# Attention logits from four products a head instead of six, and the bias table from split rows

## The chip, the cores and the metric

The kernel runs on one NeuronCore of a Trainium2 chip. The metric is the device time of one launch in microseconds (us). Engines named here: TensorE (matrix products; "PE" in the profile, its weight loads "PEld"), VectorE ("DVE"), ScalarE ("ACT") and SyncE ("SP", which only issues transfers). They run their own queues in order and wait for each other through semaphores.

## The reference

A small decoder: a retention layer, then an attention layer (MoBA), each with an MLP and a gated per-layer embedding, for 256 positions and a model width of 2048. The change concerns the attention logits alone. With 256 positions there is one block of keys, so each of 16 heads (width 128) attends causally over its own block:

```
l_own = einsum('hqd,hkd->hqk', qc, k_own) * scale          # scale = 128 ** -0.5
l_own = where(dist_own >= 0, l_own + bias_t[:, t5_bucket(dist_own)], NEG_INF)
probs = softmax(l_own)
```

`bias_t` is a table of 32 distance buckets by 16 heads. All arrays are float32.

## The kernel before

**Precision.** Each float32 operand x is split into a high part (a cast to float32r, which ScalarE does) and a low part (x minus the high part, VectorE); `split` (lines 217 to 219) does both. A product is then made of three: high x high, high x low, low x high.

**Units.** The whole kernel is a list of units. One unit is one 128 x 1024 piece of weights. `run` goes through the units in order: it issues the load of a later piece, splits the piece three units ahead (`conv`, tiles wh and wl, lines 218 and 219), issues the unit's products, and then the tasks that were put behind this unit with `at`. Nothing is rescheduled: the order of the Python calls is the order of every engine's queue.

**The attention layer** has four groups of four heads. With b the number of a group's first unit, units b to b+7 compute the keys (ak), b+8 to b+15 the queries (aq), b+16 to b+23 the values (av). `evac_q` adds the two halves of a query tile and splits it into qx (high part in columns 0 to 255, low part in 256 to 511); kx is the same for the keys. Behind unit b+11+2j stands `logits` for head j of the group, behind unit b+15+2j `turn`. So behind unit b+15 stand the evacuation of the last query tile, `turn` of the first head and `logits` of the third, in this order, and behind b+17 `turn` of the second head and `logits` of the fourth.

`logits` takes one PSUM bank and computes two blocks in it: queries 0 to 127 against keys 0 to 127 (t=0) and queries 128 to 255 against all keys (t=1), with three products each (lines 742 to 744). VectorE scales each block and adds the bias (line 751), takes the row maximum (752); ScalarE does the exponential and its sum (753); VectorE divides (754, 757). `turn` takes one bank, transposes the probabilities into it (line 764) and splits them from the bank into ph (ScalarE) and pl (VectorE), lines 218 and 219. The bank is free once pl is done.

**Banks.** `aux` hands out two banks in turn, to the logits, the transposes and some small products of other layers. A tile that gets a bank waits until the last reader of its former tile is done.

**The bias table.** `bias_rows` loads the table (33 x 16, tile relb) and a one-hot matrix (33 x 384, tile oh), multiplies them in float32 (line 677) and stores the rows; each group reads its part back as tile T.

Of the kernel before, what the change touches and what calls it, by code (L numbers as in the profile page):

```python
# [11 lines left out]
F32R = mybir.dt.float32r  # L12
I32 = mybir.dt.int32
AF = mybir.ActivationFunctionType
ALU = mybir.AluOpType
AX = mybir.AxisListType

P = 128
S = 256
# [5 lines left out]
AH, DH = 16, 128  # L25
# [44 lines left out]
class Core:  # L70
# [593 lines left out]
    def bias_rows(self, i):  # L664
        nc, cp, io = self.nc, self.cp, self.io
        st = {}

        def load():
            st["rb"] = cp.tile([33, AH], F32, name="relb")
            nc.vector.memset(st["rb"][32:33], NEG)  # L670
            nc.sync.dma_start(st["rb"][:32], io["rel_bias"])
            st["oh"] = self.slot("oh", (33, 384))
            nc.sync.dma_start(st["oh"], io["onehot"])

        def rows():
            ps = self.aux("bv")
            nc.tensor.matmul(ps[:AH, :384], st["rb"], st["oh"], start=True, stop=True)
            st["bv"] = self.slot("bv", (AH, 384))
            nc.vector.tensor_copy(st["bv"], ps[:AH, :384])

        def store():
            nc.scalar.dma_start(io["bvec"], st["bv"][:, None, :].to_broadcast([AH, BR, 384]))
        self.at(i, load)
        self.at(i + 6, rows)
        self.at(i + 8, store)

    def attention(self):
        nc = self.nc
        mm = nc.tensor.matmul
        first = len(self.units)  # L690
        self.at(first + 4, self.stats_a)
        self.at(first + 6, self.stats_b)
        sc = {}

        def q_scale():
            sc["s"] = self.cp.tile([P, 2], F32, name="qs")
            nc.vector.tensor_scalar_mul(sc["s"], self.rn, DH ** -0.5)
        self.at(first + 8, q_scale)
        self.ot = {}
        for g in range(AH // GH):  # L700
            b, st = len(self.units), {}

            def table(st=st, g=g):
                st["T"] = []
                bv = self.io["bvec"]
                for j in range(0, GH, 2):
                    t = self.slot("T", (P, 2, S))
                    for q in range(0, P, BR):
                        src = bass.AP(tensor=bv.tensor, offset=bv.offset + (g * GH + j) * BR * 384 + 127 - q, ap=[[383, BR], [BR * 384, 2], [1, S]])
                        nc.sync.dma_start(t[q:q + BR], src)  # L710
                    st["T"] += [t[:, 0], t[:, 1]]
            self.at(b, table)

            def evac_k(n, ps, st=st):
                t = self.small("kt")
                self.fold(t, ps)
                yield
                yield
                nc.vector.tensor_mul(t, t, self.rb)
                x = self.slot("kx", dt=F32R)  # L720
                self.split(x[:, :S], x[:, S:], t)
                st["k", n] = x

            def evac_q(n, ps, st=st):
                t = self.small("qt")
                self.fold(t, ps)
                yield
                x = self.slot("qx", dt=F32R)
                self.split(x[:, :S], x[:, S:], t)
                st["q", n] = x  # L730

            self.phase_a(f"ak{g}_", "att", g * 24, GH, 2, LEAD if g == 0 else 1, lambda k: self.xx[k], evac_k)
            self.phase_a(f"aq{g}_", "att", g * 24 + 8, GH, 2, 1, lambda k: self.x2[k], evac_q)

            def logits(j, st=st):
                ps = self.aux("lg")
                q, k = st["q", j], st["k", j]
                for t in range(2):
                    o = ps[:, :P] if t == 0 else ps[:, P:384]
                    n = P * (t + 1)  # L740
                    qh, ql = q[:, t * P:(t + 1) * P], q[:, S + t * P:S + (t + 1) * P]
                    mm(o, qh, k[:, :n], start=True, stop=False)
                    mm(o, qh, k[:, S:S + n], start=False, stop=False)
                    mm(o, ql, k[:, :n], start=False, stop=True)
                l = self.slot("lg", (P, 384))
                mx = self.cp.tile([P, 2], F32, name="mx", tag="mx", bufs=2)
                sm = self.cp.tile([P, 2], F32, name="sm", tag="sm", bufs=2)
                for t in range(2):
                    c = slice(0, P) if t == 0 else slice(P, 384)
                    bias = st["T"][j][:, P:] if t == 0 else st["T"][j]  # L750
                    nc.vector.scalar_tensor_tensor(l[:, c], ps[:, c], sc["s"][:, t:t + 1], bias, op0=ALU.mult, op1=ALU.add)
                    nc.vector.reduce_max(mx[:, t:t + 1], l[:, c], axis=AX.X, negate=True)
                    nc.scalar.activation(l[:, c], l[:, c], AF.Exp, bias=mx[:, t:t + 1], accum_out=sm[:, t:t + 1])
                nc.vector.reciprocal(sm, sm)
                for t in range(2):
                    c = slice(0, P) if t == 0 else slice(P, 384)
                    nc.vector.tensor_scalar_mul(l[:, c], l[:, c], sm[:, t:t + 1])
                st["p", j] = l

            def turn(j, st=st):  # L760
                p = st.pop(("p", j))
                ps = self.aux("pt")
                for i, (c, o) in enumerate(((0, 0), (1, 1), (2, 2))):
                    nc.tensor.transpose(ps[:, o * P:(o + 1) * P], p[:, c * P:(c + 1) * P], self.ident)
                h, l = self.slot("ph_", (P, 384), F32R), self.slot("pl_", (P, 384), F32R)
                self.split(h, l, ps[:, :384])
                st["t", j] = (h, l)

            def evac_v(banks, st=st):
                st["v"] = self.natural(banks, self.rn)  # L770

            def values(j, st=st, g=g):
                (vh, vl), (ph, pl) = st["v"], st["t", j]
                ps = self.bank("y", "y", 2)
                c = slice(j * P, (j + 1) * P)
                for t in range(2):
                    o = ps[:, :S] if t == 0 else ps[:, P:S]
                    p = slice(0, S) if t == 0 else slice(S, 384)
                    mm(o, vh[t][:, c], ph[:, p], start=t == 0, stop=False)
                    mm(o, vh[t][:, c], pl[:, p], start=False, stop=False)  # L780
                    mm(o, vl[t][:, c], ph[:, p], start=False, stop=t == 1)
                x = self.slot(f"o{g}_{j}", dt=F32R)
                self.split(x[:, :S], x[:, S:], ps[:, :S])
                self.ot[g * GH + j] = x

            self.phase_b(f"av{g}_", "att", g * 24 + 16, KD // 2, lambda k: self.xx[k], evac_v)
            for j in range(GH):
                self.at(b + 11 + 2 * j, lambda j=j, f=logits: f(j))
                self.at(b + 15 + 2 * j, lambda j=j, f=turn: f(j))
                self.at(b + 25 + j // 2, lambda j=j, f=values: f(j))  # L790

        self.project("att_o", "att_o", 0, KD // 2, lambda k: self.ot[k], self.add([G_MLP1]))
# [82 lines left out]
```

## Time and profile before

| | |
|---|---|
| median of 3 runs | 2763.4 us (2762.8 to 2763.84) |
| profiled execution | 2764.53 us, of which span 2762.7 us |
| TensorE busy | 2748.0 us (99%) |
| VectorE busy | 1682.7 us (61%) |
| ScalarE busy | 1310.3 us (47%) |
| chain that ended last | 99% TensorE |
| granted TensorE clock, mean | 0.999 |

The span runs from the first instruction to the last in one profiled execution; shares are of the span. The chain that ended last is followed back from the last instruction, each step to what it waited for. Matrix products are pipelined: the interval between two starts, not the duration of one, is what a product holds TensorE for.

### The profile page before, as it was taken

To read this page: it belongs to the slowest core of one execution; us is meant where nothing else is said; L and a number is where in the kernel's file an instruction comes from. 1 tells how busy PE (TensorE), PEld (TensorE's weight loads), DVE (VectorE), ACT (ScalarE), POOL (GpSimd) and SP (SyncE) were. 2 spreads that over 40 slices of the span, in tenths; PEclk is the share of its full clock that TensorE was granted. 3 is DMA by queue.
4 is the path that set the end of the run, shared out by engine and by line. 5 is a ranking of instruction groups with operands and counts; after the bars stand their busy time and mean duration, and the time that the engine had idled before them with its cause. 6 is when DMAs were issued, how large, how long until landed. Compare 5 with 4: busy or idle time off the path is not lost.

```text
span 2762.7 us, 34143 instructions
## 1 busy us (share of the span) xinstructions
PE 2748.0 (99%) x13802; PEld 2339.9 (85%) x13802; DVE 1682.7 (61%) x2264; ACT 1310.3 (47%) x1787; POOL 0.2 (0%) x4
## 2 busy tenths in 40 slices
PE   9999999999999999999999999999999999999998
PEld 7888888888888888888888888888888888888886
DVE  6766666655566544665556776665666445664555
ACT  5444444444445433444445655554554334544454
POOL 0000000000000000000000000000000000000000
PEclk9999999999999999999999999999999999999999
DMA  7555554555555555555565555554555555555554
GB/s 267 186 186 186 186 183 179 182 183 197 183 193 189 192 191 196 185 196 185 186 209 185 189 178 183 181 178 175 196 184 197 187 194 193 189 189 192 185 200 153
DMA packets 79307, 522.50 MB, mean 189 GB/s; under 512 B 8971, under 2 KB 12972, under 8 KB 17452
## 3 DMA queue, kind: packets, MB, share of 16 engines
q1 hardware_dynamic: 78476, 519.26, 52.9%
q10 hardware_dynamic: 672, 1.05, 0.3%
q8 instruction: 108, 1.77, 0.3%
q14 instruction: 51, 0.42, 0.0%
HBM read 517.39 MB, written 2.88 MB: 188 GB/s over the span
## 4 chain that ended last, share of the span: by engine, by line
PE 99%; DVE 0%; DMA 0%; ACT 0%; SPq 0%; issue 0%
PE up L154 17%; PE up L152 9%; PE qk L154 4%; PE ak L154 2%; PE aq L154 2%; PE qk L152 2%; PE ak L152 1%; PE aq L152 1%; PE pu L551 1%; PE xt L252 1%; PE qk L181 1%; PE y L439 1%; PE sc L417 0%; PE qk L182 0%; PE dn__11012 L192 0%; PE dn__11012 L194 0%
## 5 line engine op out<-in xcount | busy, mean ns | idle before, releaser
L219 DVE TENSOR_TENSOR wl<-raw,wh 128x1024 fp32r<-128x1024 f32 (+1 forms) x970 | 1179.9, 1222 | 659.6 <-ACT wh L218 645.3
L218 ACT CAST wh<-raw 128x1024 fp32r<-128x1024 f32 (+1 forms) x970 | 1015.1, 1051 | 718.2 <-DVE rs_y L275 29.2
L154 PE MATMUL up<-x,wh 128*128 128x512 f32 x2048 | 490.5, 391 | 0.0
L154 PEld LDWEIGHTS up<-x,wh 128*128 128x128 f32 x2048 | 376.0, 188 | 72.5
L152 PEld LDWEIGHTS up<-x,wl 128*128 128x128 f32 x2048 | 263.4, 191 | 10.4
L152 PE MATMUL up<-x,wl 128*128 128x256 f32 x2048 | 266.6, 283 | 0.0
L223 ACT COPY t<-up 128x256 f32<-128x256 f32 x128 | 47.6, 372 | 331.4 <-PE up L154 331.4
L224 DVE TENSOR_TENSOR t<-t,up 128x256 f32<-128x256 f32 x128 | 53.9, 421 | 216.6 <-ACT t L223 216.3
L154 PE MATMUL qk<-x,wh 128*128 128x512 f32 x448 | 109.9, 392 | 0.0
L154 PEld LDWEIGHTS qk<-x,wh 128*128 128x128 f32 x448 | 81.8, 188 | 15.5
L230 ACT ACTIVATE x<-xt,g 128x256 fp32r<-128x256 f32 x112 | 52.5, 478 | 53.3 <-DVE x L231 39.4
L231 DVE SCALAR_TENSOR_TENSOR x<-xt,g,x 128x256 fp32r<-128x256 f32 x112 | 52.9, 480 | 27.9 <-ACT x L230 27.6
L154 PE MATMUL aq<-x,wh 128*128 128x512 f32 x256 | 63.2, 391 | 0.0
L154 PE MATMUL ak<-x,wh 128*128 128x512 f32 x256 | 63.1, 392 | 0.0
L152 PEld LDWEIGHTS qk<-x,wl 128*128 128x128 f32 x448 | 57.4, 191 | 2.2
L152 PE MATMUL qk<-x,wl 128*128 128x256 f32 x448 | 58.1, 283 | 0.0
L511 DVE SCALAR_TENSOR_TENSOR s<-t 128x256 f32<-128x256 f32 x128 | 54.6, 426 | 4.4
L154 PEld LDWEIGHTS ak<-x,wh 128*128 128x128 f32 x256 | 46.6, 188 | 8.7
L154 PEld LDWEIGHTS aq<-x,wh 128*128 128x128 f32 x256 | 46.5, 188 | 8.6
L219 DVE TENSOR_TENSOR a<-s,a 128x256 fp32r<-128x256 f32 x128 | 53.7, 419 | 0.0
L218 ACT CAST a<-s 128x256 fp32r<-128x256 f32 x128 | 52.0, 406 | 0.0
L239 ACT ACTIVATE sq<-h 128x512 f32<-128x512 f32 x48 | 30.1, 628 | 37.4 <-DVE h L520 15.6
(1011 smaller groups left out, 4992.3 us busy)
## 6 DMA issues: line engine op xcount, KB each, us to landing
raw<-mlp_up SPq DMA_DIRECT2D x128, 1024.0 KB, 4.8
raw<-mlp_dn SPq DMA_DIRECT2D x128, 1024.0 KB, 4.8
raw<-ret_in SPq DMA_DIRECT2D x94, 1024.0 KB, 4.8
raw<-att SPq DMA_DIRECT2D x48, 1024.0 KB, 4.8
raw<-ret_out SPq DMA_DIRECT2D x32, 1024.0 KB, 4.8
raw<-ple_gate SPq DMA_DIRECT2D x32, 1024.0 KB, 4.8
raw<-att_o SPq DMA_DIRECT2D x16, 1024.0 KB, 4.8
raw<-ple_up SPq DMA_DIRECT2D x4, 1024.0 KB, 4.8
```

Of the source, the lines that this page charges most:

```text
L152: mm(ps[:, S:], wl[:, c], rhs[k][:, :S], start=False, stop=end)
L154: mm(ps, wh[:, c], rhs[k], start=first and k == 0, stop=end)
L181: m(ps, wh[:, c], x, start=u + j == 0, stop=False)
L218: self.nc.scalar.copy(dst_h, src)
L219: self.nc.vector.tensor_sub(dst_l, src, dst_h.bitcast(F32))
L223: self.nc.scalar.copy(dst, ps[:, :S])
L224: self.nc.vector.tensor_add(dst, dst, ps[:, S:])
L230: self.nc.scalar.activation(t[:, :S], src, AF.Copy, scale=gs)
L231: self.nc.vector.scalar_tensor_tensor(t[:, S:], src, gs, t[:, :S].bitcast(F32), op0=ALU.mult, op1=ALU.subtract)
L239: self.nc.scalar.activation(self.slot("sq"), self.h[c][:, t], AF.Square, accum_out=self.ssq[:, t, c:c + 1])
L252: self.nc.tensor.transpose(ps[:, o * P:(o + 1) * P], self.h[c][:, t, f * P:(f + 1) * P], self.ident)
L511: nc.vector.scalar_tensor_tensor(s, t, 0.0, t, op0=ALU.max, op1=ALU.mult)
```

## The change

The products of the high part of the queries with both parts of the keys become one: the moving operand is the whole kx tile (512 columns) for t=1, and its first 128 columns of either half (2 x 128) for t=0. Their two results stand side by side in a bank of their own, so each t takes a bank, and a head takes two. The product of the low part of the queries with the high part of the keys is added to the first half. VectorE then adds two halves: one operation with the bias as before, and a second that adds the other half to the result. For the bias table, the one-hot matrix is cast and the table is split by a new task two units before the product, which becomes two products.

```
--- before.py
+++ after.py
@@ -672,9 +672,17 @@
             st["oh"] = self.slot("oh", (33, 384))
             nc.sync.dma_start(st["oh"], io["onehot"])
 
+        def parts():
+            st["ohr"] = self.slot("ohr", (33, 384), F32R)
+            nc.scalar.copy(st["ohr"], st["oh"])
+            st["rh"], st["rl"] = (cp.tile([33, AH], F32R, name=n) for n in ("relh", "rell"))
+            self.split(st["rh"], st["rl"], st["rb"])
+        self.at(i + 4, parts)
+
         def rows():
             ps = self.aux("bv")
-            nc.tensor.matmul(ps[:AH, :384], st["rb"], st["oh"], start=True, stop=True)
+            nc.tensor.matmul(ps[:AH, :384], st["rh"], st["ohr"], start=True, stop=False)
+            nc.tensor.matmul(ps[:AH, :384], st["rl"], st["ohr"], start=False, stop=True)
             st["bv"] = self.slot("bv", (AH, 384))
             nc.vector.tensor_copy(st["bv"], ps[:AH, :384])
 
@@ -733,22 +741,24 @@
             self.phase_a(f"aq{g}_", "att", g * 24 + 8, GH, 2, 1, lambda k: self.x2[k], evac_q)
 
             def logits(j, st=st):
-                ps = self.aux("lg")
                 q, k = st["q", j], st["k", j]
-                for t in range(2):
-                    o = ps[:, :P] if t == 0 else ps[:, P:384]
-                    n = P * (t + 1)
+                pss = []
+                for t in range(2):
+                    ps, n = self.aux("lg"), P * (t + 1)
                     qh, ql = q[:, t * P:(t + 1) * P], q[:, S + t * P:S + (t + 1) * P]
-                    mm(o, qh, k[:, :n], start=True, stop=False)
-                    mm(o, qh, k[:, S:S + n], start=False, stop=False)
-                    mm(o, ql, k[:, :n], start=False, stop=True)
+                    x = k if t else k.rearrange("p (a s) -> p a s", a=2)[:, :, :P]
+                    o = ps if t else ps[:, :S].rearrange("p (a s) -> p a s", a=2)
+                    mm(o, qh, x, start=True, stop=False)
+                    mm(ps[:, :n], ql, k[:, :n], start=False, stop=True)
+                    pss.append((ps[:, :n], ps[:, n:2 * n]))
                 l = self.slot("lg", (P, 384))
                 mx = self.cp.tile([P, 2], F32, name="mx", tag="mx", bufs=2)
                 sm = self.cp.tile([P, 2], F32, name="sm", tag="sm", bufs=2)
                 for t in range(2):
                     c = slice(0, P) if t == 0 else slice(P, 384)
                     bias = st["T"][j][:, P:] if t == 0 else st["T"][j]
-                    nc.vector.scalar_tensor_tensor(l[:, c], ps[:, c], sc["s"][:, t:t + 1], bias, op0=ALU.mult, op1=ALU.add)
+                    for half, rest in zip(pss[t], (bias, l[:, c])):
+                        nc.vector.scalar_tensor_tensor(l[:, c], half, sc["s"][:, t:t + 1], rest, op0=ALU.mult, op1=ALU.add)
                     nc.vector.reduce_max(mx[:, t:t + 1], l[:, c], axis=AX.X, negate=True)
                     nc.scalar.activation(l[:, c], l[:, c], AF.Exp, bias=mx[:, t:t + 1], accum_out=sm[:, t:t + 1])
                 nc.vector.reciprocal(sm, sm)
```

TensorE's queue behind unit b+15 of the first group, before: `turn` of the first head (pt), then `logits` of the third (lg), then the first products of the values.

```order
L764 MATMUL pt<-ident,lg 128x128 x3
L742 MATMUL lg<-kx,qx 128x128 [waits DVE_49,Activation_49]
L743 MATMUL lg<-kx,qx 128x128
L744 MATMUL lg<-kx,qx 128x128 [waits DVE_49]
L742 MATMUL lg<-kx,qx 128x256
L743 MATMUL lg<-kx,qx 128x256
L744 MATMUL lg<-kx,qx 128x256
L192 MATMUL av_0__12998<-wh_12874,x_0_11957 128x512 [waits PE_49]
L193 MATMUL av_0__12998<-wl_12875,x_0_11957 128x512
```

The same place after. (Names in brackets are the engines' semaphores that an instruction waits for.)

```order
L774 MATMUL pt<-ident,lg 128x128 [waits DVE_49,PE_49]
L774 MATMUL pt<-ident,lg 128x128 x2
L751 MATMUL lg<-kx,qx 128x256 [waits DVE_49,PE_49,Activation_49]
L752 MATMUL lg<-kx,qx 128x128 [waits DVE_49]
L751 MATMUL lg<-kx,qx 128x512 [waits DVE_49]
L752 MATMUL lg<-kx,qx 128x256
L192 MATMUL av_0__13008<-wh_12882,x_0_11964 128x512
L193 MATMUL av_0__13008<-wl_12883,x_0_11964 128x512
L194 MATMUL av_0__13008<-wh_12882,x_0_11964 128x512
```

Six logits products became four, and the third of them, the first one in the head's second bank, has got a wait for VectorE.

VectorE's queue at the second head of the first group, before: from the evacuation of a query tile (qt) over the logits (lg, mx, sm) to the next weight piece and the low part of the third head's queries.

```order
L224 TENSOR_TENSOR qt<-qt,aq_2_12854 128x256 [waits Activation_49]
L751 SCALAR_TENSOR_TENSOR lg<-lg,qs,T 128x128 [waits PE_49]
L752 TENSOR_REDUCE mx<-lg 128x1 [waits DVE_49]
L751 SCALAR_TENSOR_TENSOR lg<-lg,qs,T 128x256
L752 TENSOR_REDUCE mx<-lg 128x1 [waits DVE_49]
L754 RECIPROCAL sm<-sm 128x2 [waits Activation_49]
L757 TENSOR_SCALAR lg<-lg,sm 128x128 [waits DVE_49]
L757 TENSOR_SCALAR lg<-lg,sm 128x256
L219 TENSOR_TENSOR wl_12919<-raw_12780,wh_12918 128x1024 [waits Activation_49]
L219 TENSOR_TENSOR qx<-qt,qx 128x256 [waits Activation_49]
```

The same place after.

```order
L224 TENSOR_TENSOR qt<-qt,aq_2_12862 128x256 [waits Activation_49]
L761 SCALAR_TENSOR_TENSOR lg<-lg,qs,T 128x128 [waits PE_49]
L761 SCALAR_TENSOR_TENSOR lg<-lg,qs 128x128 [waits DVE_49]
L762 TENSOR_REDUCE mx<-lg 128x1 [waits DVE_49]
L761 SCALAR_TENSOR_TENSOR lg<-lg,qs,T 128x256 [waits PE_49]
L761 SCALAR_TENSOR_TENSOR lg<-lg,qs 128x256 [waits DVE_49]
L762 TENSOR_REDUCE mx<-lg 128x1 [waits DVE_49]
L764 RECIPROCAL sm<-sm 128x2 [waits Activation_49]
L767 TENSOR_SCALAR lg<-lg,sm 128x128 [waits DVE_49]
L767 TENSOR_SCALAR lg<-lg,sm 128x256
L219 TENSOR_TENSOR wl_12928<-raw_12787,wh_12927 128x1024 [waits Activation_49]
L219 TENSOR_TENSOR qx<-qt,qx 128x256 [waits Activation_49]
```

Two operations were added, each behind the first of its block and waiting for it; the rest stands as before, behind them.

## Rows read from the trace of the kernel before

**Rows 1.** The page, part 1: busy us (share of the span), instructions.

```profile
PE 2748.0 (99%) x13802; PEld 2339.9 (85%) x13802; DVE 1682.7 (61%) x2264; ACT 1310.3 (47%) x1787; POOL 0.2 (0%) x4
```

**Rows 2.** Waits of TensorE: for whom, total us, times, longest us.

```profile
PE qk L181 <- ACT wh L218: 2.3, 1, 2.3
```

**Rows 3.** Timeline, TensorE, first group, third head: start us, us, engine, line, operation.

```profile
1608.17 0.28 PE L744 MATMUL lg<-kx,qx 128*128 128x128 f32 x1
1608.28 0.33 PE L742 MATMUL lg<-kx,qx 128*128 128x256 f32 x1
...
1608.57 0.28 PE L744 MATMUL lg<-kx,qx 128*128 128x256 f32 x1
1608.69 0.40 PE L192 MATMUL av__12998<-wh,x 128*128 128x512 f32 x1
```

**Rows 4.** Timeline around the bias table's product (line 677).

```profile
1393.75 0.39 PE L193 MATMUL dn__11013<-wl,a 128*128 128x512 f32 x1
...
1393.98 0.39 PE L194 MATMUL dn__11013<-wh,a 128*128 128x512 f32 x1
...
1395.04 0.19 PEld L192 LDWEIGHTS dn__11012<-wh,a 128*128 128x128 f32 x1 [0.64 <-issue]
1395.04 0.50 PE L192 MATMUL dn__11012<-wh,a 128*128 128x512 f32 x1
...
1395.38 0.39 PE L193 MATMUL dn__11012<-wl,a 128*128 128x512 f32 x1
```

**Rows 5.** Timeline, first group, fourth head.

```profile
1614.65 0.28 PE L744 MATMUL lg<-kx,qx 128*128 128x128 f32 x1
...
1615.18 0.56 DVE L219 TENSOR_TENSOR pl__13036<-pt,ph__13035 128x384 fp32r<-128x384 f32 x1 [0.16 <-ACT ph__13035 L218]
```

**Rows 6.** Timeline at the start of the kernel.

```profile
5.34 0.42 DVE L219 TENSOR_TENSOR wl<-raw,wh 128x256 fp32r<-128x256 f32 x1
5.82 0.29 PEld L182 LDWEIGHTS qk<-x,wl 128*128 128x128 f32 x1 [0.27 <-DVE wl L219]
```

**Rows 7.** Timeline, VectorE, first group, third head.

```profile
1608.73 0.55 DVE L219 TENSOR_TENSOR pl__12970<-pt,ph__12969 128x384 fp32r<-128x384 f32 x1
1609.20 0.34 DVE L751 SCALAR_TENSOR_TENSOR lg<-lg,qs,T 128x128 f32<-128x128 f32 x1
1609.58 0.29 DVE L752 TENSOR_REDUCE mx<-lg 128x1 f32<-128x128 f32 x1
1609.78 0.48 DVE L751 SCALAR_TENSOR_TENSOR lg<-lg,qs,T 128x256 f32<-128x256 f32 x1
1610.29 0.42 DVE L752 TENSOR_REDUCE mx<-lg 128x1 f32<-128x256 f32 x1
```

**Rows 8.** Waits of VectorE, 1596.6 to 1609.28 us: first head to third.

```profile
DVE sm L754 <- ACT lg L753: 1.3, 2, 0.7
DVE wl L219 <- ACT wh L218: 0.4, 2, 0.2
```

**Rows 9.** Timeline, VectorE, second group, second and third head.

```profile
1673.94 1.22 DVE L219 TENSOR_TENSOR wl<-raw,wh 128x1024 fp32r<-128x1024 f32 x1
1675.28 0.42 DVE L224 TENSOR_TENSOR qt<-qt,aq 128x256 f32<-128x256 f32 x1
...
1680.22 1.22 DVE L219 TENSOR_TENSOR wl<-raw,wh 128x1024 fp32r<-128x1024 f32 x1
1681.56 0.42 DVE L224 TENSOR_TENSOR qt<-qt,aq 128x256 f32<-128x256 f32 x1
1682.00 0.56 DVE L219 TENSOR_TENSOR pl__13670<-pt,ph__13669 128x384 fp32r<-128x384 f32 x1
```

**Rows 10.** Timeline, TensorE, second group, third head, second half.

```profile
1681.57 0.33 PE L742 MATMUL lg<-kx,qx 128*128 128x256 f32 x1
```

**Rows 11.** Two stretches, TensorE: us, busy us (products), clock, DMA, GB/s.

```profile
9.30:13.98 4.68, 4.68 (x15) 1.00 1.03 406
13.98:18.66 4.68, 4.68 (x27) 1.00 1.04 407
```

## The prediction

> **What bounds the kernel now.** I read the page's engine line first: TensorE is busy for 2748.0 us, 99% of the span [rows 1]. Then the list of what TensorE waited for: beyond the very first products it holds a single entry, 2.3 us at the start [rows 2], and nothing in the attention layer. So the kernel is a gapless queue of matrix products, executed in the order written. Whatever takes time out of that queue is gained in full; whatever makes a product wait is lost in full, because nothing later has slack to give it back. Third, the order in which TensorE's products wait in the changed program (shown with the change). Fourth, the timelines of TensorE and VectorE around the logits.
>
> **The products themselves.** Around the third head of the first group a logits product of 128 columns holds the queue for 0.11 us (1608.17 to 1608.28) and one of 256 columns for hardly more (1608.57 to 1608.69, 0.12); the three of the second half take 0.41 in all, with one short delay at the change of width [rows 3]. A product of 512 columns takes 0.23 (1393.75 to 1393.98) [rows 4]. The new four products (256, 128, 512, 256) then cost 0.11 + 0.11 + 0.23 + 0.11 against six times 0.11: one slot of 0.11 less per head, 16 x 0.11 = 1.8 us over the kernel. The weight loads saved (two per head) lie beside other products and are counted at nothing; were each to hold the queue for its own 0.19 us [rows 4], that is a rival below.
>
> [...]
>
> **The bias table.** The single-precision product of 384 columns stands between the last ordinary product at 1393.98 and the next at 1395.04, which itself takes 0.34 instead of 0.23 to the next [rows 4]. Its cost is 1395.04 - (1393.98 + 0.23) + 0.11 = 0.94 us. Two products of the kind used elsewhere, 384 columns at three quarters of 0.23, 0.17 each, and a restart of 0.11 make 0.45: a gain of 0.49, once (bounds: nothing, and 0.94 less 0.34). The two casts and one subtraction that make the split rows stand two units earlier on engines that are busy 47% and 61% [rows 1]; they cost nothing, and 0.7 us if they were in TensorE's way.
>
> **The new wait.** There are two banks of the kind "aux". Before, a head's logits took one; now they take both. At the third and fourth head of each group the transposes of an earlier head stand directly ahead and have just taken a bank too. So the third allocation in that unit, the 512-column product, must take the bank of those transposes and cannot start before ScalarE and VectorE have emptied it. The order shows exactly this: the 512-column product waits for VectorE there, and not at heads one and two. What must end is VectorE's subtraction pl<-pt. Behind the waiting product stands all of TensorE's work.
>
> How late is it? Before, at the fourth head, pl starts at 1615.18 and lasts 0.56, so it ends at 1615.74, while the second half, then the third product, could have started at 1614.65 [rows 5]. Waking TensorE took 0.06 us when it waited for VectorE at the start (the subtraction ends 5.34 + 0.42 = 5.76, the weight load starts at 5.82) [rows 6], and the product began 0.03 later. So the second half starts at 1615.83 instead of 1614.65 + 0.11 = 1614.76: 1.07 late. What follows is then 0.23 + 0.11 and a restart of 0.11 (the 0.34 instead of 0.23 above) against 0.41: 0.05 more. Fourth head: +1.12 us.
>
> [...]
>
> **What VectorE's extra work adds.** Each head now has four scalar-tensor-tensor operations instead of two, and each waits for the one before. In the trace the small one starts 0.38 before its successor (1609.20, 1609.58), the large one 0.51 before (1609.78, 1610.29) [rows 7]: the chain of a head grows by 0.38 + 0.51 = 0.89 us. Usually that would hide, with VectorE at 61%. It does not here. From the first head's logits to pl of the third head VectorE of the first group waits only for ScalarE's steps of the same chain: 1.3 + 0.4 us, none for TensorE [rows 8]. So two heads' growth, 1.78 us, arrives in full at pl: it ends at 1608.73 + 0.55 + 1.78 = 1611.06 instead of 1609.28 [rows 7]. With 0.09 to wake, the second half of the third head starts at 1611.15 instead of 1608.28: 2.87 late, and 0.05 for restart and the shorter remainder: +2.92. This includes shorter waits on the way (at head two the low part of its queries, itself a VectorE result, comes some 0.6 us late); they add nothing, since the end is set by VectorE's chain. At the fourth head VectorE is later by 1.78 + 0.89 less 0.16 of idle time [rows 5] = 2.51, less than TensorE's 2.92: TensorE leads again, and the +1.12 stands. First group: 4.04 us.
>
> In the second group (the third's and fourth's lists of VectorE's waits read the same) VectorE has a little slack: each row may start 0.09 before the previous one ends (1608.73 + 0.55 and 1609.20 in [rows 7]), so 1673.94 + 1.22 - 0.09 = 1675.07 against 1675.28 is 0.21 idle; 1680.22 to 1681.56 another 0.21; 1681.56 to 1682.00 another 0.11 [rows 9]. The growth reaching pl is 1.78 - 0.53 = 1.25; it ends at 1682.00 + 0.56 + 1.25 = 1683.81, the second half starts at 1683.90 instead of 1681.57 [rows 10]: 2.33, with 0.05 and 1.12 it is 3.50 a group. Three such groups: 10.50.
>
> **Sum.** 4.04 + 10.50 - 0.49 = +14.05 us; the 0.11 saved per head is inside (heads one and two gain nothing, as VectorE sets the end). The profiled execution took 2764.53 us (span 2762.7 and 1.8 around it), 1.1 more than the median 2763.4: 2764.53 + 14.05 - 1.1 = 2777.5 us, 0.5% slower.
>
> Unknown in it: the second addition reads the same bank and SBUF instead of the bias tile; I take the first's price. From half of it (0.45 a head; the wait at the third head falls by 0.9 a group) to half more, the sum runs from 10.5 to 17.6. Two runs of 128 columns as one moving operand stand nowhere in the trace: from 0.11 (256 columns) to 0.23 (512), at most 1.9 us over 16, and half of that hides behind VectorE.
>
> **Rivals.**
> 1. The direct wait alone: VectorE's growth hides (it catches up, as its idle time of 39% suggests [rows 1]; its waits speak against it [rows 8]). Then 8 x 1.12 - 8 x 0.11 for heads one and two - 0.49 = +7.6: 2771.0. Chance 0.14.
> 2. Not slower: the bank is free when asked for, because the allocator hands out another one than the transposes'. The waits vanish and only the saving is left: -1.8 - 0.5 = -2.3, 2761.1, within what can be told from no change. For it: TensorE never waited before [rows 2]. Against: the order's wait. It decides once the wait at the 512-column product is for anything but pl. Chance 0.05.
> 3. Faster: banks free, and each weight load saved gives back its own time, 32 x 0.19 = 6.0, and 0.5: 2756.9. Against: products start every 0.11 us, so loads of 0.19 must overlap [rows 3, 4]. Chance 0.03.
> 4. The pace falls after each wait. [...] Chance 0.06.
>
> **How the numbers follow.** The forecast has 0.72: 2777.5, by its own unknowns 2774 to 2781. The range reaches down to rival 1 and up past the forecast's own upper end, since the restart and wake-up prices come from single rows: 2770.5 to 2783. Rivals 2 to 4, 0.14 in all, stay outside. A measurement of this kernel tells 0.2% (5.5 us) from no change. Slower: forecast, rivals 1 and 4, 0.72 + 0.14 + 0.06 = 0.92; within: rival 2, 0.05; faster: rival 3, 0.03.
>
> **What would show it.** In the profile after, TensorE's waits should list the 512-column logits product behind VectorE's pl eight times, about 1.7 us at third heads and 1.1 at fourth heads, and the 128-column product at second heads behind VectorE's qx a few tenths; VectorE's recip to recip distance should grow by 0.9 before the third head; the granted clock should stay 1.00. If TensorE shows no waits there, the bank argument is wrong; if third and fourth heads wait alike, the VectorE term is.

## The result and the profile after

The changed kernel takes 2784.61 us (median of 6 runs, 2780.8 to 2785.07) against 2763.62 (6 runs, 2762.8 to 2764.41): 1.0074 times as long, 95% interval [1.0064, 1.0084]. It is slower, as forecast, but by 21.0 us where 14.05 were forecast, and outside the range by 1.6 us.

The profiled execution took 2784.97 us, 20.44 more than that of before. Its page says little: TensorE is busy 99% of the span again [rows 1], and the chain is 96% TensorE.

```profile
span 2783.2 us, 34132 instructions
PE 2756.5 (99%) x13770; PEld 2342.4 (84%) x13770; DVE 1696.0 (61%) x2297; ACT 1311.2 (47%) x1789; POOL 0.2 (0%) x4
```

The list of TensorE's waits, which held one product of the start [rows 2], now says nearly all. Columns: engine, operation, line, for whom; total us, times, longest us.

```profile
PE qk L181 <- ACT wh L218: 2.0, 2, 1.5
PE lg L751 <- DVE pl__12979 L219: 1.6, 1, 1.6
...
PE lg L752 <- DVE qx L219: 1.4, 5, 0.6
PE lg L751 <- DVE pl__14454 L219: 1.0, 1, 1.0
PE lg L751 <- DVE pl__13046 L219: 1.0, 1, 1.0
```

Eight waits for pl, four of 1.6 us and four of 1.0 (one of the first kind and two of the second are shown), and five for the low part of the queries (0.6 at the second head of the first group, 0.2 at each third head). They come to 11.8 us. The list counts a wait from the end of the product before it; what the queue loses runs from the moment at which the next product could have started, and is 0.1 to 0.3 us more for each. So these waits and the slow stretches below do not add up to the growth; the table of starts further on does. The timeline of the first group's third head, TensorE, answers to [rows 3]: start, duration, engine, line, operation.

```profile
1607.71 0.49 PE L774 MATMUL pt<-ident,lg 128*128 128x128 f32 x3
1607.95 0.36 PE L751 MATMUL lg<-kx,qx 128*128 128x256 f32 x1
1608.52 0.33 PE L752 MATMUL lg<-kx,qx 128*128 128x128 f32 x1 [0.21 <-DVE qx L219]
1610.46 0.53 PE L751 MATMUL lg<-kx,qx 128*128 128x512 f32 x1 [1.61 <-DVE pl__12979 L219]
1610.80 0.40 PE L752 MATMUL lg<-kx,qx 128*128 128x256 f32 x1
1611.00 0.63 PE L192 MATMUL av__13008<-wh,x 128*128 128x512 f32 x1
1611.42 0.63 PE L193 MATMUL av__13008<-wl,x 128*128 128x512 f32 x1
...
1614.32 0.40 PE L194 MATMUL av__13008<-wh,x 128*128 128x512 f32 x1
1614.56 0.40 PE L192 MATMUL av__13009<-wh,x 128*128 128x512 f32 x1
```

The 512-column product waits behind the transposes, as the order had shown. What the forecast did not have stands below it: the values' products follow each other every 0.42 us (1611.00, 1611.42) instead of 0.23, until 1614.56. The stretches of 4.1 us behind the four third-head waits, and behind the first group's fourth-head wait, TensorE: stretch, us, busy us and number of products, granted clock, DMA share, GB/s.

```profile
1610.46:1614.56 4.10, 4.10 (x12) 0.58 0.41 174
1688.86:1692.96 4.10, 4.10 (x12) 0.58 0.44 184
1767.24:1771.34 4.10, 4.10 (x11) 0.58 0.42 176
1845.65:1849.76 4.11, 4.11 (x12) 0.58 0.43 179
...
1619.63:1623.73 4.10, 4.10 (x18) 1.00 0.03 10
```

The granted clock averages 0.58 behind each third head: in the first group 0.50 for 3.41 us (1610.79 to 1614.20) and 1.00 in the rest of the stretch. Behind the fourth head it is 1.00. In the first group nine products take 1614.56 - 1611.00 = 3.56 us instead of 9 x 0.2275 = 2.05, and the product before them 0.20 instead of 0.11: 1.6 us. In each of the other three groups the nine products take 3.65 us, again 1.60 too long.

VectorE at the third head, to be read beside [rows 7]:

```profile
1609.85 0.55 DVE L219 TENSOR_TENSOR pl__12979<-pt,ph__12978 128x384 fp32r<-128x384 f32 x1
1610.32 0.34 DVE L761 SCALAR_TENSOR_TENSOR lg<-lg,qs,T 128x128 f32<-128x128 f32 x1
1610.70 0.35 DVE L761 SCALAR_TENSOR_TENSOR lg<-lg,qs 128x128 f32<-128x128 f32 x1
1611.09 0.29 DVE L762 TENSOR_REDUCE mx<-lg 128x1 f32<-128x128 f32 x1
1611.29 0.48 DVE L761 SCALAR_TENSOR_TENSOR lg<-lg,qs,T 128x256 f32<-128x256 f32 x1
1611.80 0.48 DVE L761 SCALAR_TENSOR_TENSOR lg<-lg,qs 128x256 f32<-128x256 f32 x1
1612.32 0.42 DVE L762 TENSOR_REDUCE mx<-lg 128x1 f32<-128x256 f32 x1
```

The second additions cost 0.39 and 0.52 from start to start, 0.91 a head (forecast 0.89).

A table of starts gives the sum without any model: the first product of the keys (ak) in each group, and the first of att_o behind the last, in the profiled execution of each kernel, us from the span's start. The growth against before is that of the whole attention layer.

| kernel | group 1 | group 2 | group 3 | group 4 | att_o | layer | growth |
|---|---|---|---|---|---|---|---|
| before | 1560.19 | 1632.23 | 1705.53 | 1778.82 | 1852.12 | 291.93 | |
| after | 1559.48 | 1637.20 | 1715.59 | 1794.01 | 1872.41 | 312.93 | +21.00 |
| own bank | 1559.08 | 1633.20 | 1708.02 | 1782.82 | 1857.62 | 298.54 | +6.61 |
| one addition | 1559.79 | 1634.13 | 1709.46 | 1784.79 | 1860.13 | 300.34 | +8.41 |
| wait filled | 1558.85 | 1634.94 | 1711.80 | 1788.62 | 1865.40 | 306.55 | +14.62 |
| spaced | 1559.83 | 1631.24 | 1704.15 | 1777.07 | 1849.98 | 290.15 | -1.78 |
| before, spaced | 1559.74 | 1631.48 | 1704.84 | 1778.19 | 1851.54 | 291.80 | -0.13 |
| addition alone | 1558.98 | 1632.74 | 1707.18 | 1781.61 | 1856.03 | 297.05 | +5.12 |

After, the four groups grew by 5.68, 5.09, 5.13 and 5.10 us. The forecast had 4.04 and 3.50 for each of the others. The excess is 1.64, 1.59, 1.63 and 1.60: the same 1.6 in each group that the slow stretch costs. The delay of the third heads can be read in the same way, ahead of any slow product. Counted from the group's first key product, the second half of the third head's logits starts 50.98 us in (1610.46 - 1559.48) instead of 48.09 (1608.28 [rows 3] - 1560.19) in the first group, and 51.66 (1688.86 - 1637.20) instead of 49.34 (1681.57 [rows 10] - 1632.23) in the second: 2.89 and 2.32 late, where 2.87 and 2.33 were forecast.

### The profile page after: what moved, and what is told of

The parts are those of the page before. It is cut to its first block, busy times and chain, and to the rows that moved or that the text cites. A ratio compares the mean times of both kernels' runs of the same rounds, so it can differ in the third digit from the quotient of the medians.

```text
span 2783.2 us, 34132 instructions
## 1 busy us (share of the span) xinstructions
PE 2756.5 (99%) x13770; PEld 2342.4 (84%) x13770; DVE 1696.0 (61%) x2297; ACT 1311.2 (47%) x1789; POOL 0.2 (0%) x4
## 4 chain that ended last, share of the span: by engine, by line
PE 96%; DVE 2%; ACT 1%; issue 1%; DMA 0%; SPq 0%
PE up L154 17%; PE up L152 9%; PE qk L154 4%; PE ak L154 2%; PE qk L152 2%; PE ak L152 1%; PE aq L154 1%; PE pu L551 1%; PE xt L252 1%; PE y L439 1%; PE qk L181 1%; DVE wl L219 1%; DVE lg L761 0%; PE aq L152 0%; ACT wh L218 0%
```

## The experiments

All were compared with the kernel before on the same chip: 2763.68 us for the first four below, 2763.82 us for the spaced pair and the last.

**The second block's bank from another pair.** Edit, in the changed kernel:

```
-                    ps, n = self.aux("lg"), P * (t + 1)
+                    ps, n = (self.bank("lg", "y", 2) if t else self.aux("lg")), P * (t + 1)
```

> The changed kernel, with the second block's bank (t=1) taken from the pair that the values use later, so that no logits product needs a bank of the transposes. Theory (bank wait, VectorE's longer chain, and a slower clock after the long wait at third heads): the eight waits for pl are gone and the clock stays at 1.00, but VectorE's 0.89 us more per head still delays the low part of the queries, so TensorE waits for qx at heads two to four, 0.3 to 1.2 us each, about 6.7 us in all; less 0.3 for the bias table: 2770. Rival A (the bank is the whole cause): no waits, 2761.5. Rival B (the two-run operand or the four products are slower by themselves): 2784 as before.

Measured: 2770.18 us, ratio 1.0024 [1.0015, 1.0033]. Waits of TensorE in the layer:

```profile
PE lg L752 <- DVE qx L219: 4.6, 9, 0.8
```

No wait for pl is left, the granted clock is 0.998 over the run (0.996 in the changed kernel), the values' products behind the first group's third head follow every 0.23 us, and VectorE's longer chain alone makes nine waits for the low part of the queries. So the wait for pl is the bank's, and the bank is not the whole cause.

**Without the second addition.** Edit, in the changed kernel:

```
-                    for half, rest in zip(pss[t], (bias, l[:, c])):
-                        nc.vector.scalar_tensor_tensor(l[:, c], half, sc["s"][:, t:t + 1], rest, ...)
+                    nc.vector.scalar_tensor_tensor(l[:, c], pss[t][0], sc["s"][:, t:t + 1], bias, ...)
```

> The changed kernel without VectorE's second addition (it leaves out the product of the high queries with the low keys from the sum). Theory: VectorE's chain is as long as in the kernel before, so third heads wait like fourth heads, 1.1 to 1.3 us, eight waits for pl, 8.5 us in all, less 0.3: 2771.8 if the clock stays up after waits of this length, as it did at fourth heads. Rival A (any wait at a third head brings the clock down, whatever its length): 2778. Rival B (VectorE's extra operations play no part): waits of 1.6 and 2784.

Measured: 2772.52 us, ratio 1.0032 [1.002, 1.0044]. Waits of TensorE for pl at the third and the fourth head of the first group, and the stretch behind the third head:

```profile
PE lg L751 <- DVE pl__12975 L219: 1.1, 1, 1.1
...
PE lg L751 <- DVE pl__13040 L219: 1.0, 1, 1.0
```

```profile
1608.94:1613.04 4.10, 4.10 (x18) 1.00 0.43 182
```

Third heads now wait as fourth heads do, so the other 0.5 us of their wait came from VectorE's extra operations, and so did the 0.2 us for qx just ahead of it, which is gone too. And idle time of 1.1 us at the same place leaves the clock at 1.00 (18 products in 4.1 us): it is the amount of idle time, not the place, that the slow pace goes with. Whether 1.6 us alone would do, without the 0.2 ahead of it, was not tested.

**The bias table alone.** The kernel before with `parts` and the two products of `rows`, as in the diff of the change.

> The kernel before with only the bias table's part of the change. Theory: 0.3 to 0.5 us less around that product, 2763.2, not to be told from no change; no wait anywhere. Rival (the extra casts hold up a weight piece): a wait of TensorE for wh or wl near 1390 us and 0.5 us or more lost.

Measured: 2763.34 us, ratio 0.9999 [0.9989, 1.0009]: no difference that can be told, and no wait of TensorE behind the start. The saving itself is read from the profile after, beside [rows 4]:

```profile
1393.46 0.39 PE L194 MATMUL dn__11013<-wh,a 128*128 128x512 f32 x1
1393.78 0.35 PE L684 MATMUL bv<-ohr,relh 33*16 33x384 f32 x1
1393.96 0.34 PE L685 MATMUL bv<-ohr,rell 33*16 33x384 f32 x1
1394.23 0.50 PE L192 MATMUL dn__11012<-wh,a 128*128 128x512 f32 x1
1394.56 0.39 PE L193 MATMUL dn__11012<-wl,a 128*128 128x512 f32 x1
```

1394.23 - (1393.46 + 0.23) + 0.10 = 0.64 us instead of 0.94: 0.30 saved (forecast 0.49). The same rows in the run with the bias table alone give 0.64 as well.

**The wait filled with products.** Edit, in the changed kernel, ahead of each block's first product:

```
+                    if t and j == 2:
+                        junk = self.bank("junk", "y", 2)
+                        for i in range(8):
+                            mm(junk, k[:, :P], k, start=True, stop=True)
```

> The changed kernel with eight products of 512 columns put in the wait at each third head (0.23 us each, 1.8 in all, results never used), ahead of the product that waits. Theory (idle time at third heads brings TensorE's clock down): the wait is filled, the stretch behind it runs at full pace, 6.4 us come back, less 4 times 0.2 for the filling that lasts longer than the wait: 2779. Rival (the slow pace behind third heads has another cause, such as the banks or VectorE reading them): the pace stays halved for 3.6 us, 2785.

Measured: 2778.36 us, ratio 1.0054 [1.0039, 1.0069]. TensorE at the first group's third head, and its clock behind it:

```profile
1608.03 2.07 PE L754 MATMUL junk<-kx 128*128 128x512 f32 x8
1609.94 0.39 PE L755 MATMUL lg<-kx,qx 128*128 128x512 f32 x1
1610.17 0.28 PE L756 MATMUL lg<-kx,qx 128*128 128x256 f32 x1
1610.28 0.40 PE L192 MATMUL av__13017<-wh,x 128*128 128x512 f32 x1
```

```profile
1610.40:1614.50 4.10, 4.10 (x20) 1.00 0.30 126
```

The useful product starts no earlier relative to the head than before (1609.94 - 1607.87 = 2.07 behind the second product, in the changed kernel 1610.46 - 1608.52 = 1.94), yet the products behind it run at full pace (20 in 4.10 us behind the first group's third head; the granted clock reads 1.00 over 1559 to 1875 us, where the changed kernel has 0.98), and 6.3 us come back. The idle time itself brought the clock down: 0.58 behind the third head with it, 1.00 with the products in its place. With it gone, the layer's growth is 14.62 us against the forecast's 14.54. That they agree so closely is in part luck: the filling lasts 0.13 us longer than the wait at each third head, and saves the restart of 0.11 (1609.94 to 1610.17 is 0.23).

**Heads three units apart.** Edit, in the changed kernel (and, as a control, in the kernel before):

```
-                self.at(b + 11 + 2 * j, lambda j=j, f=logits: f(j))
-                self.at(b + 15 + 2 * j, lambda j=j, f=turn: f(j))
-                self.at(b + 25 + j // 2, lambda j=j, f=values: f(j))
+                self.at(b + 11 + 3 * j, lambda j=j, f=logits: f(j))
+                self.at(b + 15 + 3 * j, lambda j=j, f=turn: f(j))
+                self.at(b + 25 + (j + 1) // 2, lambda j=j, f=values: f(j))
```

> The changed kernel with the heads of a group three units apart instead of two (logits behind units b+11, 14, 17, 20, transposes behind b+15, 18, 21, 24), so that no transposes stand in a unit with logits and VectorE has half as much time again per head. Theory (bank of the transposes taken just before, VectorE's chain without slack): no wait of TensorE in the attention layer, clock 1.00, and only the saving is left, 1.8 us for the products and 0.3 for the bias table: 2761.5, 2 us faster than the kernel before. Rival (the waits come with the two banks or the two operands themselves): 2770 or more. Rival for the size of the saving (products cost by their columns, so four cost as much as six): 2763.3.

> The kernel before with the heads three units apart, the control of the spaced version. Theory: TensorE had no waits to lose, so nothing changes: 2763.6. Rival (spacing saves time by itself, so that the spaced version's gain is not the products'): 2762 or less.

Measured: 2762.4 us, ratio 0.9995 [0.9986, 1.0003], and for the control 2763.86 us, ratio 1.0 [0.9991, 1.0009]. TensorE waits nowhere behind the start in either. In the spaced version the second head of the first group reads:

```profile
1603.79 0.28 PE L751 MATMUL lg<-kx,qx 128*128 128x256 f32 x1
1603.90 0.22 PE L752 MATMUL lg<-kx,qx 128*128 128x128 f32 x1
1603.97 0.46 PE L751 MATMUL lg<-kx,qx 128*128 128x512 f32 x1
1604.26 0.28 PE L752 MATMUL lg<-kx,qx 128*128 128x256 f32 x1
1604.38 0.40 PE L152 MATMUL aq<-x,wl 128*128 128x256 f32 x2
```

The four products hold TensorE for 0.59 us (1603.79 to 1604.38). The layer is 1.78 us shorter than before and 1.65 shorter than the control's, near the 1.8 of the forecast's first term. The version beats the changed kernel by 22 us; against the kernel before, its 1.4 us lie within what can be told from none. The time alone lies midway between the theory's 2761.5 and the 2763.3 of the rival for the size; only the table's starts tell them apart.

**The addition alone.** The kernel before with one more operation behind each of the two of a head; it adds the block times zero:

```
+                    nc.vector.scalar_tensor_tensor(l[:, c], ps[:, c], 0.0, l[:, c], op0=ALU.mult, op1=ALU.add)
```

> The kernel before with one more VectorE operation of the same shape behind each of the two per head (it adds the block times zero), six products and one bank as before. Theory (VectorE's queue has no slack between the heads, so its 0.89 us per head reach TensorE by the low part of the queries): waits for qx at heads two to four of each group, none for pl, about 6.7 us: 2770.3, clock 1.00. Rival (VectorE's extra work is hidden, and only the bank makes TensorE wait): 2763.6, no waits.

Measured: 2768.79 us, ratio 1.0018 [1.0009, 1.0027], the layer 5.12 us longer. TensorE waits for qx (2.8 us in 5 waits) and never for pl. VectorE's third head:

```profile
1609.57 0.34 DVE L751 SCALAR_TENSOR_TENSOR lg<-lg,qs,T 128x128 f32<-128x128 f32 x1
1609.94 0.29 DVE L752 SCALAR_TENSOR_TENSOR lg<-lg 128x128 f32<-128x128 f32 x1
1610.27 0.29 DVE L753 TENSOR_REDUCE mx<-lg 128x1 f32<-128x128 f32 x1
...
1610.98 0.42 DVE L752 SCALAR_TENSOR_TENSOR lg<-lg 128x256 f32<-128x256 f32 x1
1611.44 0.42 DVE L753 TENSOR_REDUCE mx<-lg 128x1 f32<-128x256 f32 x1
```

The direction is the theory's: VectorE's growth is not hidden, and without a second bank it makes TensorE wait for qx instead. The size is 1.5 us below what I expected. With a constant instead of a column as its factor the added operation takes 0.33 and 0.46 from start to start, 0.79 a head and not 0.89, so it is a weaker dose; that this explains all of the 1.5 was not tested.

## Why the prediction was wrong, point by point

- **What bounds the kernel: right.** TensorE's queue had no slack; all that was lost in it was lost in the time.
- **The products: right.** 1.8 us forecast; in the spaced version, where nothing waits, 1.78 against the kernel before and 1.65 against the control. Had products cost by their columns, the rival for the size in the spaced version, four would have cost as much as six, which this does not show. The price of 0.11 for every product of 128 columns was too simple all the same: at heads one and two of the kernel before the first of a head's three holds the queue for 0.06 us in six cases of eight (1601.38 to 1601.44, say), and behind the transposes of the first group's third head for 0.15.
- **The bias table: too large a gain,** 0.30 instead of 0.49, within its bounds. The 0.7 us for the casts and the subtraction, were they in TensorE's way, was the author's estimate without a row; in the profile after they took 0.51, 0.20 and 0.16 us on their own engines, and TensorE waited for none of them.
- **The new wait: right** in place, count and reason; at third heads the second half came 2.89 and 2.32 us late, as forecast. At the fourth head it comes 1.09 late (1619.63 instead of 1618.43 + 0.11; forecast 1.07), which the list, counting from the end of the product before, shows as 1.0, and the restart behind it is there (1619.63 to 1619.97 is 0.34). The wait for qx, expected at second heads, is listed at one second head and at all four third heads. Weight load and product started together behind the wait:

```profile
1618.43 0.22 PE L752 MATMUL lg<-kx,qx 128*128 128x128 f32 x1
...
1619.63 0.19 PEld L751 LDWEIGHTS lg<-kx,qx 128*128 128x128 f32 x1 [1.13 <-DVE pl__13046 L219]
1619.63 0.50 PE L751 MATMUL lg<-kx,qx 128*128 128x512 f32 x1 [0.98 <-DVE pl__13046 L219]
...
1619.97 0.28 PE L752 MATMUL lg<-kx,qx 128*128 128x256 f32 x1
```

  So the weights were not loaded during the wait, and the restart was paid: 0.34 us to the next product instead of 0.23, as where load and product start together at 1395.04 in [rows 4].
- **VectorE's extra work: right.** 0.91 a head instead of 0.89, and from the first group's first reciprocal to its second 6.98 us (1598.98 to 1605.96) instead of 6.06 (1598.79 to 1604.85), where 0.9 more was forecast. Without it (one addition) the third heads' waits fall from 1.6 to 1.1; without the wait for the bank (own bank) the layer is still 6.61 us longer. The first group lost more than the others, as forecast from its missing slack.
- **The sum: wrong by one term.** The step that failed is the one that left TensorE's clock at 1.00 behind the waits. It stood in the prediction as rival 4, "The pace falls after each wait", with 0.06. It came true at four of the eight waits, the long ones, at 1.6 us each. No run shows the 2.1 us a wait that [rows 11] suggest as its price (an estimate: 15 products in the 4.68 us behind the start's 2.3 us wait, 27 in the next 4.68, and 12 of 27 x 4.68 = 2.1). Those rows show no fall behind the wait either. At that start a 512-column product holds the queue for 0.42 us ahead of the wait (6.20 to 6.62) as well as behind it (10.14 to 10.56), so that wait did not bring the pace down:

```profile
6.20 0.63 PE L181 MATMUL qk<-x,wh 128*128 128x512 f32 x1
6.62 0.41 PE L182 MATMUL qk<-x,wl 128*128 128x256 f32 x1
```

  But this is the pace that the changed kernel shows at a granted clock of 0.50, so the 1.00 that the column reads at the start [rows 11] is no ground to leave the clock out. The sum now: 14.54 + 4 x 1.6 = 20.9 against the layer's 21.00. Less 0.30 for the bias table and 0.26 less elsewhere that is the 20.44 between the profiled executions; the start's wait, 2.0 instead of 2.3, is part of the 0.26.
- **Rivals 1 to 3** did not happen. Rival 2's price, 2.3 us faster, is nearly what the spaced version saves in its layer and its table (1.78 + 0.30), where the waits are taken away by other means.
- **The range** left rival 4 outside as a whole. A part of it, the four longest waits at the price of rows 11, would have reached 2777.5 + 4 x 2.1 = 2786.

One run of the six took 2780.8 us at a mean clock of 0.997, where the profiled one had 0.996. Fewer falls of the clock would explain it, but a run of 2783.53 us reads 0.997 too, and no profile shows either run, so this stays open.

## What to carry to other kernels

A bank is not free because it is one of a pair: count, in queue order, who took it last, and whether that tile can be empty by then; here it was not, and TensorE waited 1.6 us at each third head and 1.0 at each fourth. Where one engine is the bound, a longer chain on a half-idle engine need not be hidden: here VectorE, 61% busy, had at most 0.53 us of idle time in its chain up to a third head [rows 9], and with the second block's bank from another pair, so without any wait for it, the layer still grew by 6.61 us. Look for whom the chain waits in that stretch, not at its engine's share of the span. And price a new wait of TensorE with what the clock does behind it, here 1.6 us more behind each wait of 1.6: where waits must be, shorten them (at 1.0 and 1.1 us the clock stayed at 1.00) or take them apart by spacing the work, since the same work three units apart took 2762.4 us, against 2763.82 before.

## What was not expected of the hardware

Waits of 1.6 us (behind one of 0.2) in an otherwise gapless queue brought the granted clock to 0.58 over the following 4.1 us, four times of four in the profiled execution, and cost as much again as the wait itself (1.6 us each); waits of 1.0 and 1.1 us left it at 1.00 and cost nothing beyond themselves but the restart (0.34 us to the next product instead of 0.23). In the first group the clock is still 1.00 when the wait ends at 1610.46 and falls to 0.50 at 1610.79, so it is the work behind the wait that pays. Products without use, put in the wait, kept the clock at 1.00 (20 products in 4.10 us behind it instead of 12).
